# Up projection of a gated MLP as seven Strassen block products, and the down projection as a stage of its own

## The chip, the cores and the metric

The kernel runs on one core of one Trainium2 chip. The metric is the device time of one execution in microseconds (us): 1302.23 us, the median of three runs that lie between 1301.54 and 1302.39 us.

## The reference

One layer of a diffusion backbone: a token mixer (four recurrent heads and four Fourier groups) with a gated residual, then a gated MLP with a gated residual, then a last norm. The latents are 1024 tokens of 1024 features, all float32. The change lies in the MLP and around it:

```python
x = x + gt1 * (y @ w_out[l])
h2 = modulate(rms_norm(x, norm2[l]), sh2, sc2)
# conv_ffn, D_FF = 2816 hidden features, grid of 16 rows x 64 columns
a, u = jnp.split(h2 @ w_up, 2, axis=-1)
a = depthwise_conv_3x3(a) + b_dw
x = x + gt2 * ((jax.nn.gelu(a) * u) @ w_down)
return rms_norm(x, norm_f)
```

## The kernel before

Features lie on the 128 partitions and tokens along them. A page is a tile of 128 x 1024 float32. Every large product is done in three passes of TensorE: each operand is split into a rounded high part and the rest (ScalarE casts, line 62; VectorE subtracts, line 63), and high x high, high x low and low x high are summed in PSUM (`mm3`, line 76; `half_T`, line 285; all matmuls are recorded at line 74). A matmul has 128 columns of weights and 512 tokens.

`out_proj` (line 709) goes over the tokens in two halves and over eight feature tiles in each; it adds the residual into eight pages `x1` that stay in SBUF (line 727), sums squares, and then norms and modulates the half (`token_rstd` line 95, `row_bcast` line 103, `modulated` line 108) into the pages `h2`. While the second half is normed, TensorE does products of the first up projection with tokens of the first half (`half_T` on `up0`).

`ffn` (line 756) goes over 22 pairs `ff` of column tiles: 128 gate columns a and 128 columns u. Each is a product over eight feature tiles and two token halves, so 2 x 8 x 2 x 3 = 96 matmuls of 512 tokens a pair. The gate goes from PSUM into SBUF (line 774) and gets the centre tap on ScalarE (line 775), eight shifted taps on VectorE (line 783), GELU (line 785) and the product with u (line 793); the product is split for the next matmul. After every second pair, `down` (line 803) multiplies the two tiles by their rows of `w_down`: 96 matmuls, and 16 sums into `x1` on VectorE (line 812). The last group of two pairs is done in 512, 256 and 256 tokens, each followed by the last norm, transposes (line 835) and the store (`final`, line 816).

GpSimd does nothing in these stages. All transfers are issued from SyncE's queue (line 59). The order of the instructions on each engine is made when the program is built, by a list scheduler that takes the earliest ready instruction in program order; weight loads and their splits are put ahead (`wload` with `ahead`, line 65). At run time each engine follows its list in order.

Of the kernel before, what the change touches and what calls it, by code (L numbers as in the profile page):

```python
# [16 lines left out]
P = 128  # L17
D = 1024
L = 1024
# [15 lines left out]
class Kern:  # L35
# [59 lines left out]
    def token_rstd(self, ssacc, ntt, name, ptag="m"):  # L95
        """ssacc [128 features, ntt*128 tokens] -> rstd [128 tokens, ntt]"""
# [6 lines left out]
    def row_bcast(self, r, ntt, pt, off=0):  # L103
        """pt[:, off+j*128+t] = r[t, j] on every partition"""
# [11 lines left out]
    # ------------------------------------------------------------------ set-up  # L116
    def consts(self):
# [9 lines left out]
        self.mscan = c.tile([P, L], U8, tag="mscan", name="mscan")  # L127
# [5 lines left out]
        # for the first two rows of the modulation: stationary operands of 32 columns, two of them in use  # L133
# [8 lines left out]
        z = lambda n: c.tile([P, 512], F32, tag=n, name=n)  # L142
# [25 lines left out]
    def masks(self):  # L168
        nc, c = self.nc, self.sb["cst"]
# [9 lines left out]
    def mod_pair(self, ft):  # L179
        """shift and scale of feature tile ft for the first norm, of the latents and of the context"""  # L180
# [27 lines left out]
    def mod_part(self, part):  # L208
        """part 0..3: gt1, sh2, sc2, gt2"""
# [26 lines left out]
    # ------------------------------------------------------------------ first norm, zi  # L236
    def start(self):
        """The first norm in halves of 512 tokens; the values of the recurrent heads"""
# [22 lines left out]
        def square_sum(tiles, w, tag="sq"):  # L261
            """the last tile in pieces of w, which are added to the sum of the others"""
# [41 lines left out]
        # the clock of the tensor engine rises only when it is busy  # L304
# [52 lines left out]
        # context  # L357
# [38 lines left out]
    def half_T(self, pt, w, half, kts=(0, NK)):  # L396
        """one half of the tokens of an up projection, feature tiles kts"""
# [65 lines left out]
        # direction 0: half u of each chunk in row u; direction 1: in row 1 - u  # L463
# [8 lines left out]
        # states at the end of the context  # L472
# [42 lines left out]
        # scores  # L515
# [15 lines left out]
        # keys decayed to the end, queries from the start of each pair of chunks  # L531
# [10 lines left out]
        # chunk contributions to the states  # L542
# [20 lines left out]
        # outputs [tokens, values]  # L563
# [44 lines left out]
    def fnet(self):  # L608
# [27 lines left out]
        for g in range(4):  # L636
# [24 lines left out]
            # even and odd part; the last three rows mirror the rows 1 to 3 with the odd part negated  # L661
# [16 lines left out]
    # ------------------------------------------------------------------ gate of the recurrent heads  # L678
# [29 lines left out]
    # ------------------------------------------------------------------ output projection, second norm  # L708
    def out_proj(self):
        nc, V, I = self.nc, self.nc.vector, self.I  # L710
        self.x1 = [self.pg() for _ in range(NK)]
        order = [4, 5, 6, 7, 0, 1, 2, 3]
        h2 = None
        for half in range(2):
            s = slice(half * 512, (half + 1) * 512)
            ssacc = None
            for d in range(NK):
                if half == 0:
                    self.load(self.x1[d], I["xT"][d])
# [7 lines left out]
                V.scalar_tensor_tensor(self.x1[d][:, s], pt, self.gt1[:, d:d + 1], self.x1[d][:, s], op0=MUL, op1=ADD)  # L727
                sq = self.pg(F32, "zt")
                nc.scalar.activation(sq[:, :512], self.x1[d][:, s], AF.Square)
# [4 lines left out]
            if half == 1:  # L734
                w0 = [self.wload(I["wup"][0, 0], "pg", "pg"), self.wload(I["wup"][0, 1])]
                self.up0 = [self.pst("g"), self.pst("g")]
                self.half_T(self.up0[0], w0[0], 0)
            r = self.token_rstd(ssacc[:, :512], 4, "n2", "c")
            if half == 1:
# [223 lines left out]
```

## Time and profile before

| | |
|---|---|
| median of three runs | 1302.23 us |
| the profiled execution, first to last instruction (span) | 1301.3 us |
| TensorE matmuls, busy | 1265.0 us (97%) |
| VectorE, busy | 849.5 us (65%) |
| ScalarE, busy | 463.1 us (36%) |
| GpSimd, busy | 0.2 us (0%) |
| HBM traffic | 92.24 MB read, 4.19 MB written |

The profile is of one execution; its own time is the span, and the median of the runs lies 0.9 us above it. Matmuls overlap in the records, so TensorE's pace is read from the distance between starts, or from the length of an unbroken row of them. Weight loads are listed apart (PEld) and run beside the matmuls.

### The profile page before, as it was taken

How to read it: one execution, taken by the hardware profiler on the slowest of the kernel's cores; microseconds unless marked ns; L12 is line 12 of the kernel's file. 1: busy time of each engine (PE TensorE's matmuls, PEld its weight loads, DVE VectorE, ACT ScalarE, POOL GpSimd, SP SyncE). 2: the span in 40 equal slices, each digit the busy share in tenths (PEclk: the TensorE clock that was granted, in tenths of full speed). 3: DMA queues.
4: the chain of work that ended last, by engine and by line, in shares of the span. 5: the costliest groups of instructions: out<-in, count | busy, mean ns of one | idle time of the engine just before them, and what ended most of it. 6: DMA issues, size and time to landing. Idle time of an engine off the chain costs nothing.

```text
span 1301.3 us, 15784 instructions
## 1 busy us (share of the span) xinstructions
PE 1265.0 (97%) x6508; PEld 1060.9 (82%) x6508; DVE 849.5 (65%) x1172; ACT 463.1 (36%) x657; POOL 0.2 (0%) x4
## 2 busy tenths in 40 slices
PE   7999999999989999999999999999999999999996
PEld 4688887888988888888888888888888888888886
DVE  5843848476975664768656565656565656565776
ACT  6534463727132443444131313131313131313336
POOL 0000000000000000000000000000000000000000
PEclk9999999999999999999999999999999999999999
DMA  9531101101362354312121212121112121212103
GB/s 333 199 97 58 33 17 33 33 17 59 104 210 75 122 176 157 100 63 65 33 65 33 66 33 65 33 65 33 65 33 65 33 65 33 65 33 65 33 1 129
DMA packets 32503, 97.45 MB, mean 75 GB/s; under 512 B 3504, under 2 KB 3760, under 8 KB 32432
## 3 DMA queue, kind: packets, MB, share of 16 engines
q1 hardware_dynamic: 32432, 96.45, 22.7%
q8 instruction: 51, 0.84, 0.2%
q14 instruction: 20, 0.16, 0.0%
HBM read 92.24 MB, written 4.19 MB: 74 GB/s over the span
## 4 chain that ended last, share of the span: by engine, by line
PE 77%; ACT 10%; DVE 7%; DMA 3%; issue 2%; SPq 0%; DVEq 0%; ACTq 0%
PE psg L74 45%; PE psm L74 30%; DMA wm<-in_wm_dram 2%; DVE pg L459 1%; ACT sq L576 1%; ACT pg L822 1%; ACT L452 1%; ACT L453 1%; DMA ld<-in_wm_dram 1%; ACT zt L821 1%; ACT wh L62 1%; DVE ma L220 1%; ACT k L470 1%; ACT pg L452 1%; DVE zt L783 1%
## 5 line engine op out<-in xcount | busy, mean ns | idle before, releaser
L74 PE MATMUL psg<-pg,wh 128*128 128x512 f32 x1784 | 484.8, 391 | 0.6 <-ACT zt L775 0.6
L74 PEld LDWEIGHTS psg<-pg,wh 128*128 128x128 f32 x1784 | 333.4, 188 | 68.8 <-ACT zt L775 1.0
L74 PE MATMUL psg<-pg,wl 128*128 128x512 f32 x892 | 279.8, 391 | 0.0
L783 DVE SCALAR_TENSOR_TENSOR zt<-zt,vec,zt 128x945 f32<-128x945 f32 (+2 forms) x176 | 214.7, 1220 | 20.9 <-ACT zt L775 17.4
L63 DVE TENSOR_TENSOR wl<-wr,wh 128x1024 fp32r<-128x1024 f32 x79 | 96.6, 1223 | 193.8 <-ACT wh L62 192.6
L74 PEld LDWEIGHTS psg<-pg,wl 128*128 128x128 f32 x892 | 167.3, 188 | 34.1
L62 ACT CAST wh<-wr 128x1024 fp32r<-128x1024 f32 x79 | 82.9, 1050 | 304.9 <-PE psg L74 249.3
L812 DVE SCALAR_TENSOR_TENSOR pg<-psm,gt,pg 128x512 f32<-128x512 f32 (+1 forms) x184 | 130.2, 724 | 14.1 <-PE psm L74 12.9
L74 PE MATMUL psm<-gx,wd 128*128 128x512 f32 x480 | 135.1, 389 | 0.2 <-DVE gx L63 0.2
L74 PE MATMUL psm<-pg,wd 128*128 128x512 f32 x480 | 134.9, 389 | 0.0
L74 PEld LDWEIGHTS psm<-gx,wd 128*128 128x128 f32 x480 | 90.0, 188 | 19.2 <-DVE gx L63 0.6
L74 PEld LDWEIGHTS psm<-pg,wd 128*128 128x128 f32 x480 | 90.1, 188 | 18.7
L74 PE MATMUL psg<-wh,pg 128*128 128x256 f32 x512 | 97.5, 289 | 0.9 <-ACT wh L62 0.8
L62 ACT CAST wd<-wr 128x1024 fp32r<-128x1024 f32 x20 | 21.1, 1054 | 193.2 <-PE psm L74 164.3
L74 PEld LDWEIGHTS psg<-wh,pg 128*128 128x128 f32 x512 | 81.6, 194 | 1.6 <-ACT wh L62 1.3
L74 PE MATMUL psg<-wl,pg 128*128 128x256 f32 x256 | 73.7, 289 | 3.9 <-DVE wl L63 3.9
L74 PE MATMUL psm<-pg,pg 128*128 128x128 f32 (+2 forms) x328 | 71.8, 342 | 5.0 <-DVE pg L514 4.7
L74 PEld LDWEIGHTS psm<-pg,pg 128*128 128x128 f32 x328 | 51.9, 190 | 14.1 <-DVE pg L514 6.1
L74 PE MATMUL psg<-pg,pg 128*128 128x512 f32 x240 | 59.0, 395 | 1.2 <-ACT pg L113 1.2
L220 DVE SCALAR_TENSOR_TENSOR ma<-wm,silu_c,ma 128x512 f32<-128x512 f32 x56 | 42.0, 750 | 19.5 <-DMA wm<-in_wm_dram 19.2
L74 PEld LDWEIGHTS psg<-pg,pg 128*128 128x128 f32 x240 | 44.2, 188 | 12.6 <-ACT pg L113 2.2
L74 PEld LDWEIGHTS psg<-wl,pg 128*128 128x128 f32 x256 | 49.6, 194 | 4.6 <-DVE wl L63 4.5
(262 smaller groups left out, 1319.1 us busy)
## 6 DMA issues: line engine op xcount, KB each, us to landing
wr<-in_wup_dram SPq DMA_DIRECT2D x44, 512.0 KB, 3.5
wm<-in_wm_dram SPq DMA_DIRECT2D x64, 256.0 KB, 3.0
wr<-in_wd_dram SPq DMA_DIRECT2D x22, 512.0 KB, 3.5
ld<-in_wm_dram SPq DMA_DIRECT2D x16, 512.0 KB, 8.2
wr<-in_wo_dram SPq DMA_DIRECT2D x16, 512.0 KB, 3.5
pg<-in_xT_dram SPq DMA_DIRECT2D x12, 512.0 KB, 6.8
wr<-in_wT_dram SPq DMA_DIRECT2D x12, 512.0 KB, 3.6
out_dram<-wr SPq DMA_DIRECT2D x8, 512.0 KB, 2.6
```

Of the source, the lines that this page charges most:

```text
L62: self.nc.scalar.copy(hi, raw)
L63: self.nc.vector.tensor_tensor(lo, raw, hi.bitcast(F32), op=SUB)
L74: self.nc.tensor.matmul(out, lhsT, rhs, start=start, stop=stop)
L220: nc.vector.scalar_tensor_tensor(acc, w, s, acc, op0=MUL, op1=ADD)
L452: nc.scalar.activation(lf, g[d][0], AF.Ln)
L453: nc.scalar.activation(self.sm(1, "tab"), lf[:, 0:1], AF.Exp) # loads the table ahead
L459: V.tensor_tensor_scan(flip(lf, d), flip(lf, d), self.mscan, 0.0, op0=ADD, op1=MUL)
L470: nc.scalar.activation(kv[d], nat(st[d]["lf"]), AF.Exp, scale=-1.0)
L576: nc.scalar.activation(sq, o[:, blk(n)], AF.Square, accum_out=self.ssq[:, h * NT + n:h * NT + n + 1])
L783: V.scalar_tensor_tensor(c3[:, ro, co], a3[:, ri, ci], w9((dr + 1) * 3 + dc + 1), c3[:, ro, co], op0=MUL, op1=ADD)
L812: self.nc.vector.scalar_tensor_tensor(x[:, s], pt, self.gt2[:, d:d + 1], x[:, s], op0=MUL, op1=ADD)
L821: nc.scalar.activation(sq[:, :w], x[:, s], AF.Square)
```

## The change

For each pair, the weights are a 2 x 2 array of blocks: a or u, times the first or second 512 features. The normed input is a 2 x 2 array too: features halves times token halves (B11, B12, B21, B22). Their product is formed with seven block products instead of eight, in the form with shared sums: S1 to S4 are sums of weight blocks, U1 to U4 of input blocks. One block product is 4 x 3 = 12 matmuls of 512 tokens.

- `out_proj` keeps the residual stream in half pages that are written to DRAM (`x1d`, eight stores of 512 KB) and read back at the end. `norm2` forms raw blocks, splits of B11, B21, B22, and U1 to U4 with their splits. The pools of the MLP are opened between the halves' end and the second norm, and the first two products of pair 0 are issued ahead of that norm.
- `up_load` loads a pair's weights, forms the sums on GpSimd (four additions of 128 x 512 and one subtraction of 128 x 1024), and splits them.
- `ffn` does the seven products into three PSUM banks, with three copies to SBUF on ScalarE and three sums on VectorE. The gate stays in PSUM and the taps read it there. The gated page goes to DRAM (`gd`, 22 stores of 512 KB).
- `down` runs after all pairs: it loads gated halves back and splits them, and sums over all 22 pairs in PSUM. The first token half goes in two sweeps over four feature tiles with 512 tokens (528 matmuls), the second in two sweeps over eight feature tiles with 256 tokens (1056 matmuls), each with its own load and split of the weights. `final` follows each part.
- Tables of the recurrence stage move to a pool that is closed before the MLP. Comments are gone.

```diff
+    def norm2(self, half, xs, ssacc):
...
+            self.phase("ffn")
+            self.up_first()
+        r = self.token_rstd(ssacc[:, :512], 4, "n2", "g")
...
+        for j in range(2):
+            b12 = block("B12", j, 2 * j, False)
+            b22 = block("B22", j, 4 + 2 * j)
+            u1, u2 = self.pg(F32, "cv"), self.pg()
+            V.tensor_tensor(u1, self.raw["B11"][j], b12, op=SUB)
+            V.scalar_tensor_tensor(u2, u1, -1.0, b22, op0=MUL, op1=SUB)
+            operand("U2", u2)
+            operand("U1", u1)
...
+            G.tensor_tensor(s31[:, hi], u[:, lo], u[:, hi], op=ADD)
+            G.tensor_tensor(s24[:, lo], s31[:, hi], a[:, lo], op=ADD)
+            G.tensor_tensor(s24[:, hi], s24[:, lo], a[:, hi], op=ADD)
+            G.tensor_tensor(s31[:, lo], a[:, lo], u[:, lo], op=ADD)
+            S24 = self.pg(F32R, "sh"), self.pg(F32R, "sl")
+            self.split(s24, *S24)
+            S31 = self.pg(F32R, "sh"), self.pg(F32R, "sl")
+            nc.scalar.copy(S31[0], s31)
+            G.tensor_tensor(S31[1], s31, S31[0].bitcast(F32), op=SUB)
+            A22 = self.tile([P, 512], F32R, "ah"), self.tile([P, 512], F32R, "al")
+            self.split(u[:, hi], *A22)
...
+                X, Y = self.pst("m"), self.pst("m")
+                self.product(X, w["A11"], "B11", True)
+                s1 = snap(X)
+                self.product(Y, w["A12"], "B21", True)
+            pa = self.pst("g")
+            V.tensor_tensor(pa[:, h0], s1, Y, op=ADD)
+            self.product(X, w["S2"], "U2", False)
+            sv = snap(X)
+            Z = self.pst("m")
+            self.product(Z, w["S1"], "U1", True)
+            s5 = snap(Z)
+            self.product(X, w["S3"], "U3", False)
+            u = self.pg(F32, "uu")
+            V.scalar_tensor_tensor(u[:, h1], X, -1.0, s5, op0=MUL, op1=SUB)
+            self.product(Z, w["S4"], "B22", False)
+            V.tensor_tensor(pa[:, h1], sv, Z, op=ADD)
+            self.product(X, w["A22"], "U4", False)
+            nc.scalar.mul(u[:, h0], X, -1.0)
             if ff + 1 < NF:
-                nxt = [self.wload(I["wup"][ff + 1, j]) for j in range(2)]
-            if len(pend) == 2 and ff < NF - 2:
-                self.down(pend)
+                self.upw.append(self.up_load(ff + 1))
+            cv = self.pg(F32, "cv")
...
-            nc.scalar.copy(a, pa)
             nc.scalar.activation(cv, pa, AF.Identity, bias=v[:, V_BDW + ff:V_BDW + ff + 1], scale=w9(4))
...
+            V.tensor_tensor(cv, cv, u, op=MUL)
+            g = self.tile([P, 1024], F32, "gd")
+            self.load(g, cv)
+            self.gd.append(g)
+        self.down()
...
-    "ffn": (dict(zt=5, wd=4, gx=4), dict(m=4)),
+    "ffn": (dict(wx=2, ws=2, sh=2, sl=2, ah=1, al=1, cv=2, uu=1, sn=4), dict(m=4)),
```

In the last lines the numbers are buffers: one page for u (`uu`), two for the gate (`cv`), two each for the split sums (`sh`, `sl`, one pair's worth), two for raw sums (`ws`). The general pool of pages has 30, before and after.

## Rows read from the trace of the kernel before

**Rows 1.** The page of the profile, part 1: span and engines
```profile
span 1301.3 us, 15784 instructions
...
PE 1265.0 (97%) x6508; PEld 1060.9 (82%) x6508; DVE 849.5 (65%) x1172; ACT 463.1 (36%) x657; POOL 0.2 (0%) x4
```

**Rows 2.** The chain that ended last, in order of time: start us, us, engine, lines
```profile
617.20 20.93 PE psm L74 x91
638.13 43.52 PE psg L74 x192
681.65 21.76 PE psm L74 x96
```

**Rows 3.** Who waited for whom between 640 and 1236 us, longest first: top rows
```profile
ACT wh L62 <- PE psg L74: 203.9, 36, 9.3
DVE wl L63 <- ACT wh L62: 166.8, 27, 9.6
```

**Rows 4.** Busy time of the engines in stretches
```profile
core 0: us, PE busy (x) PEld busy (x) DVE busy (x) ACT busy (x) POOL busy (x), PEclk, DMA share, GB/s
488.00:560.00 72.00, 71.91 (x326) 59.63 (x327) 45.26 (x63) 28.20 (x37) 0.00 (x0) 1.00 0.40 129
...
640.00:770.00 130.00, 130.00 (x575) 107.69 (x574) 82.64 (x85) 32.59 (x32) 0.00 (x0) 1.00 0.16 49
1259.00:1301.30 42.30, 32.11 (x221) 28.39 (x219) 29.24 (x65) 29.49 (x56) 0.00 (x0) 0.93 0.24 100
```

**Rows 5.** TensorE's timeline around the second norm
```profile
558.49 5.60 PE L74 MATMUL psg<-pg,pg 128*128 128x512 f32 x24
563.93 1.05 PE L74 MATMUL psc<-ones,zt 128*128 128x128 f32 x8
```

**Rows 6.** Groups of instructions by line and shape, ScalarE: busy us, mean ns
```profile
L62 ACT CAST wh<-wr 128x1024 fp32r<-128x1024 f32 x79 | 82.9, 1050 | 304.9 <-PE psg L74 249.3 <-PE psm L74 39.7 <-issue 11.5
...
L775 ACT ACTIVATE zt<-psg,vec 128x1024 f32<-128x1024 f32 x22 | 26.6, 1209 | 0.0
...
L785 ACT ACTIVATE zt<-zt 128x1024 f32<-128x1024 f32 x22 | 23.3, 1058 | 30.7 <-DVE zt L783 30.6
```

**Rows 7.** VectorE's timeline around the second norm and the first pairs
```profile
568.73 2.06 DVE L112 SCALAR_TENSOR_TENSOR zt<-pg,a,psc 128x512 f32<-128x512 f32 x3 [1.31 <-PE psc L74]
...
585.19 8.79 DVE L783 SCALAR_TENSOR_TENSOR zt<-zt,vec,zt 128x960 f32<-128x960 f32 x7
```

**Rows 8.** Groups of instructions by line and shape again, VectorE
```profile
L812 DVE SCALAR_TENSOR_TENSOR pg<-psm,gt,pg 128x512 f32<-128x512 f32 x168 | 122.8, 747 | 12.8 <-PE psm L74 11.7
...
L63 DVE TENSOR_TENSOR wl<-wr,wh 128x1024 fp32r<-128x1024 f32 x79 | 96.6, 1223 | 193.8 <-ACT wh L62 192.6
...
L459 DVE TENSOR_TENSOR_SCAN pg<-pg,mscan 128x1024 f32<-128x1024 f32 x8 | 18.3, 2292 | 11.2 <-ACT tab L453 11.2
...
L510 DVE SCALAR_TENSOR_TENSOR k<-zt,oml,k 128x512 f32<-128x512 f32 x16 | 11.6, 745 | 0.0
...
L733 DVE TENSOR_TENSOR zt<-zt,zt 128x512 f32<-128x512 f32 x14 | 9.6, 686 | 0.1
```

**Rows 9.** DMA issues on the page: KB each, us to landing
```profile
wr<-in_wup_dram SPq DMA_DIRECT2D x44, 512.0 KB, 3.5
...
out_dram<-wr SPq DMA_DIRECT2D x8, 512.0 KB, 2.6
```

**Rows 10.** TensorE's timeline in the last group: start us, us, line, shape, count
```profile
1289.70 0.52 PE L74 MATMUL psm<-pg,pg 128*128 128x256 f32 x3
1290.06 0.53 PE L74 MATMUL psm<-gx,pg 128*128 128x256 f32 x3
1290.42 1.33 PE L835 MATMUL psg<-ident,pg 128*128 128x128 f32 x10
```

**Rows 11.** The page of the profile, part 2: GB/s in 40 slices of the span
```profile
GB/s 333 199 97 58 33 17 33 33 17 59 104 210 75 122 176 157 100 63 65 33 65 33 66 33 65 33 65 33 65 33 65 33 65 33 65 33 65 33 1 129
```

More of the change, by code (lines that the diff above doesn't have):

```diff
@@ L168, in masks @@
     def masks(self):
-        nc, c = self.nc, self.sb["cst"]
+        nc, c = self.nc, self.sb["cm"]
         mk = self.pg(F32, "ld")[:, :4 * P]
@@ L742, in out_proj @@
[L742 to L753 removed]
+                if d % 2:
+                    t = self.x1d[half, d // 2] = self.tile([P, 1024], F32, "x1d")
+                    self.load(t, x)
@@ new lines, in up_load @@
+    def up_load(self, ff):
+        nc, I, G = self.nc, self.I, self.nc.gpsimd
+        lo, hi = slice(0, 512), slice(512, 1024)
+        with self.tc.high_priority():
+            a, u = self.pg(F32, "wr"), self.pg(F32, "wx")
+            self.load(a, I["wup"][ff, 0])
+            self.load(u, I["wup"][ff, 1])
+            A = self.pg(F32R, "wh"), self.pg(F32R, "wl")
+            self.split(a, *A)
+            s24, s31 = self.pg(F32, "ws"), self.pg(F32, "ws")
+            G.tensor_tensor(s31[:, hi], u[:, lo], u[:, hi], op=ADD)
[9 more added lines that the diff above has]
+            self.split(u[:, hi], *A22)
+        cut = lambda t, s: (t[0][:, s], t[1][:, s])
+        return dict(A11=cut(A, lo), A12=cut(A, hi), S2=cut(S24, lo), S4=cut(S24, hi), S3=cut(S31, lo), S1=cut(S31, hi),
+                    A22=A22)
@@ new lines, in product, with up_first @@
+    def product(self, out, w, name, first):
+        B = self.B[name]
+        for kt in range(4):
+            q, t = slice(kt * P, (kt + 1) * P), slice((kt % 2) * 512, (kt % 2 + 1) * 512)
+            for j, (a, b) in enumerate(((0, 0), (0, 1), (1, 0))):
+                self.nc.tensor.matmul(out, w[a][:, q], B[kt // 2][b][:, t], start=(first and kt == 0 and j == 0),
+                                      stop=(kt == 3 and j == 2), skip_group_check=not first)
+    def up_first(self):
+        self.upw = [self.up_load(ff) for ff in range(1)]
+        self.upp = []
+        for w in self.upw:
+            X, Y = self.pst("m"), self.pst("m")
+            self.product(X, w["A11"], "B11", True)
+            self.product(Y, w["A12"], "B21", True)
+            self.upp.append((X, Y))
@@ new lines, in ffn, with copied, g_load @@
+            g = self.tile([P, 1024], F32, "gd")
+            self.load(g, cv)
+            self.gd.append(g)
+        self.B = None
+        self.down()
+    def copied(self, dst, src):
+        self.nc.scalar.copy(dst, src)
+        return dst
+    def g_load(self, half):
+        gs = []
+        for i in range(NF // 2):
+            raw = self.pg(F32, "ws")
+            for j in range(2):
+                self.load(raw[:, j * 512:(j + 1) * 512], self.gd[2 * i + j][:, half * 512:(half + 1) * 512])
+            hi, lo = self.pg(F32R), self.pg(F32R)
+            self.split(raw, hi, lo)
+            gs.append((hi, lo))
+        return gs
@@ new lines, in sweep, with step @@
+    def sweep(self, pages, load, pts, g, t, cut):
+        tail = []
+        n = len(pages)
+        def step(i, hi, lo, j):
+            c = pages[i][1]
+            for k in range(c * i, c * i + c):
+                gh, gl = g[k // 2]
+                tt = slice((k % 2) * 512 + t.start, (k % 2) * 512 + t.stop)
+                w = cut(k, j)
+                for m, (a, b) in enumerate(((hi, gh), (hi, gl), (lo, gh))):
+                    bank0 = len(pts) == 4 or j % 2 == 0
+                    nc = self.nc
+                    nc.tensor.matmul(pts[j], a[:, w], b[:, tt], start=(k == 0 and m == 0 and bank0),
+                                     stop=(k == NF - 1 and m == 2), skip_group_check=len(pts) != 4)
+        for i in range(n):
+            hi, lo = load(i)
+            if i < n - 2:
+                for j in range(len(pts)):
+                    step(i, hi, lo, j)
+            else:
+                tail.append((i, hi, lo))
+        for j in range(len(pts)):
+            for i, hi, lo in tail:
+                step(i, hi, lo, j)
@@ new lines, in resid, with final @@
+    def resid(self, x, pt, d):
+        self.nc.vector.scalar_tensor_tensor(x, pt, self.gt2[:, d:d + 1], x, op0=MUL, op1=ADD)
+    def final(self, xs, t0, w):
+        nc, V = self.nc, self.nc.vector
+        ssacc = self.pg(F32, "cv")[:, :w]
+        for d, x in enumerate(xs):
+            if d == 0:
+                nc.scalar.activation(ssacc, x, AF.Square)
+            else:
+                sq = self.pg(F32, "cv")[:, :w]
+                nc.scalar.activation(sq, x, AF.Square)
+                V.tensor_tensor(ssacc, ssacc, sq, op=ADD)
+            nc.scalar.activation(x, x, AF.Copy, scale=self.vec[:, V_NF + d:V_NF + d + 1])
+        tag = "g" if w == 512 else "m"
+        r = self.token_rstd(ssacc, w // P, "nf", tag)
+        for i in range(w // P):
+            t = slice(i * P, (i + 1) * P)
+            ob = self.pg(F32, "uu")
+            for h in range(2):
+                pt = self.pst(tag)[:, :512]
+                for j in range(4):
+                    nc.tensor.transpose(pt[:, j * P:(j + 1) * P], xs[4 * h + j][:, t], self.ident)
+                o = ob[:, h * 512:(h + 1) * 512]
+                if h:
+                    V.tensor_scalar(o, pt, r[:, i:i + 1], None, op0=MUL)
+                else:
+                    nc.scalar.activation(o, pt, AF.Copy, scale=r[:, i:i + 1])
+            self.load(self.out[t0 // P + i], ob)
```

219 lines of the change are left out of this document (124 added, 95 removed).

## The prediction

> **What bounds the kernel now.** First the page: TensorE is busy 97% of the span, VectorE 65%, GpSimd not at all [rows 1]. A busy TensorE need not be the limit, so the chain that ended last comes next: from 617 us on it is one unbroken row of matmuls, 192 of a pair of up projections in 43.52 us, then 96 of a down group in 21.76 us, and so on to the last group [rows 2]. Both give 0.2267 us a matmul of 512 tokens. The list of waits agrees: the long ones are ScalarE and VectorE waiting for TensorE, and TensorE is not among the waiters [rows 3]. The stretches say the same: 130.00 us of 130 at the full granted clock, VectorE at 82.64 [rows 4]. So from 558.49 us, the first matmul of the up projection [rows 5], to the end, time is counted in matmuls, and the change pays only by removing some of them while nothing else becomes late. Before that point nothing changes on TensorE: it is busy 71.91 of 72 us in the output projection [rows 4], with VectorE at 45.26 and ScalarE at 28.20, and the eight extra half-page ScalarE passes for raw blocks of the first half (each under a page cast's 1.05 us [rows 6]) and the stores of 512 KB fit beside that. I cost them at nothing; without that cover they would cost at most 8 us.
>
> **The up projection.** Removed: 12 of 96 matmuls in each of 22 pairs, 264 x 0.2267 = 59.8 us. What remains is 84 x 0.2267 = 19.04 us a pair, 418.9 us in all. The question is whether the other engines keep up with 19.04 us, since the 10.88 us of down matmuls that used to lie beside each pair are gone from this stage.
>
> VectorE per pair: eight taps, which seven in a row show at 8.79 us together [rows 7], so 10.0 us for eight. They now read PSUM; a 512-column form of this operation takes 747 ns from PSUM and 745 ns from SBUF [rows 8], so I add nothing. Three page-wide subtractions or products (splits of the a weights and of S2/S4, the gate product) at 1.223 us: 3.7. Three half-page ones (the split of A22, two sums into the gate) at 0.686: 2.1. One half-page sum for u, 0.75. Together 16.5 of 19.04 us, 87%. The sums into `x1` are gone from here. ScalarE has three page casts, one half-page cast, four half-page PSUM copies, the centre tap 1.21 and GELU 1.06 [rows 6]; with a half page taken as high as a page it would still be under 11 us.
>
> Throughput holds, so the chain matters. VectorE, in order, must finish for pair n: the second gate sum after the sixth product (0.69), then the centre tap on ScalarE (1.21), eight taps (10.0), with the split of A22 (0.69) and of a later a (1.22) between them, GELU (1.06), the gate product (1.22). Only then is the single page for u free, and the u row of pair n+1 (0.75) must have read its bank before the seventh product of n+1 may write it. That is 16.8 us plus some 0.4 for handing over between engines: 17.2, where TensorE allows 19.04. The slack is 1.8 us.
>
> GpSimd has no row here that shows an addition. Bounds: at least VectorE's own time for the same sizes [rows 8], 4 x 0.686 + 1.223 = 4.0 us a pair; at most the slowest page-wide form on VectorE, the scan at 2.292 us a page [rows 8], 4 x 1.15 + 2.29 = 6.9 us. I take the upper end, so that a slow engine is not overlooked. Either way it fits into 19 us: the raw sums have two buffers and are formed a pair ahead. By the Trainium skill (GPSIMD Engine Reference, "Elementwise — side-by-side cycle accounting") an addition of 2048 float32 takes 4497 ns there, an estimate of 6.7 us for these five; the sum would be the same. What GpSimd can cost is delay to VectorE. If each of the split of S2/S4 and the split of A22, which come right when GpSimd starts its next sums, waits about half a microsecond, the slack is nearly used up; I take a loss of 0.4 us a pair, 9 us, between 0 and 2 us a pair (0 to 44).
>
> The three copies of partial sums must be done before the next write into the same bank, one product or 2.72 us later; a half-page copy needs well under a page cast's 1.05 us, so they cost nothing unless ScalarE is held behind another wait. SyncE has three transfers a pair in place of three: two weight loads, 3.5 us to landing, and a store like the output's, 2.6 us [rows 9]. Loads queued behind a store that waits for the gate product are a pair ahead, which covers them.
>
> **The start.** Before, TensorE went on with first-half products while the second half was normed. Now it has two products, 24 x 0.2267 = 5.44 us, then the norm's small matmuls at 563.93 [rows 5]; VectorE begins to modulate at 568.73 [rows 7], as before. From there it does 12 half-page passes (three take 2.06 us [rows 7]: 8.2 us), eight page sums for U1 to U4 and eight subtractions for their splits (16 x 1.22 = 19.5), and splits of S2/S4 and A22 (1.9): 29.6 us, to 598.3. The last half of the seventh product ends 1.4 us later, at 599.7. Matmuls alone would have ended at 558.5 + 19.04 = 577.5, so 22.2 us are lost; one product of pair 1 (2.7 us) can be done in the gap, as a fourth bank is free. Loss 19.5 us; at least 10 if more is brought forward and passes overlap, at most 27 if casts on ScalarE come into the row.
>
> **The step to the down stage.** After the sixth product of the last pair VectorE still has taps, GELU wait and product, some 14 us; TensorE has the seventh product, 2.7, and, with the first gated pages and weights split ahead, one page of 24 matmuls, 5.4. The next split of weights comes behind the taps. I take 5 us lost, between 0 and 11 (14 less 2.7). The last gated page needs its store and load back, some 6 us [rows 9], and is not used before the tenth page, 49 us on.
>
> **The down stage.** First half: 528 x 0.2267 = 119.7 us. Second half: 1056 of 256 tokens. In the last group of before, three of these start every 0.36 us [rows 10], 0.12 us each, more than half of 0.2267: 126.7 us. VectorE has a gated split and a weight split in each 5.44 us, or one weight split in 2.88 us, so it is covered. A weight page of 512 KB in 2.88 us is 182 GB/s; the first slice of before moved 333 [rows 11], so I cost the loads, which each go out ahead into four buffers, at nothing. Ahead of the last part go 48 transposes and small matmuls, at 0.13 us each [rows 10] some 7 us. From the last product at 1290.59 us the tail of before took 10.7 us to the end of the span [rows 1, 10]; the new one has the same steps with 256 tokens: 11 us.
>
> **The sum.** 558.5 + 418.9 + 19.5 + 9 + 5 + 119.7 + 126.7 + 7 + 11 = 1275.3 us against the profiled span of 1301.3, the profiled execution's own time. The median of the runs is 0.9 us more, so 1276 us.
>
> **Rivals.** *All of it fits.* The chain keeps its 1.8 us slack, and start and step cost 14 and 2 in place of 19.5 and 5: 1276 - 9 - 8.5 = 1258 us. For it: VectorE has 87% of a pair and the plain rows are start to start a little shorter than their durations. Against: 1.8 of 19 us is little for a chain that changes engines five times in every pair.
>
> *VectorE's chain becomes the bound, with GpSimd in its way.* Four VectorE operations a pair read two pages of SBUF (three splits, the gate product). If each waits for one GpSimd addition of half a page, 1.15 us by the scan's row, the chain is 17.2 + 4.6 = 21.8 us, 2.8 over TensorE, 61 us in 22 pairs in place of my 9: 1276 + 52 = 1328 us, slower. It decides from a pair of about 20.7 us on, where the 26 us and the 9 us allowed are gone (35/22 = 1.6 over 19.04). For it: the slack is small. Against: the taps, the largest part, read one operand from PSUM, and the sums are bunched in under half of a pair. Beside it stands a rule of the Trainium skill (SBUF — State Buffer, "SBUF: two separate sides"): the port pair that VectorE and GpSimd share is an exclusive lock, taken by a VectorE operation with two SBUF inputs or by a GpSimd one for its whole length, and the other blocks. No run here shows it yet.
>
> *The edges eat the gain.* The start at 27 and the step at 11, and the second half's first gated pages late by as much again (11): 1276 + 7.5 + 6 + 11 = 1300 us, no change. For it: pages are tight (28 of 30 hold the input blocks). Against: gated pages come free one by one in the second sweep.
>
> **Chances.** About 0.2% of the time, 2.6 us, is what a measurement of this kernel can tell from no change. Forecast 0.56, all fits 0.18, VectorE's chain 0.17, edges 0.09, of which 0.03 a little faster, 0.04 the same and 0.02 a little slower. Faster 0.77, same 0.04, slower 0.19. The range takes in the case that all fits with 5 us below it, and upwards a loss of 1.7 us a pair: 1253 to 1305; outside stay most of the chain's case and a corner below.
>
> **What would show it.** Right: 264 fewer matmuls of 512 in the stage, a pair every 19.0 to 19.6 us in the chain, TensorE idle some 20 us between 565 and 600, VectorE above 80% in the stage, 0.12 us a matmul in the last 127 us. Wrong: a chain through VectorE's taps in every pair, subtractions of a page well above 1.22 us beside GpSimd, pairs of 20.7 us or more, or gaps of over 10 us between the stages.

## The result, and the profile after

The changed kernel takes 1310.36 us, the median of four runs between 1310.10 and 1313.72 us. The kernel before, run beside it, takes 1302.31 us (1301.54 to 1305.28, four runs). The ratio is 1.0064, with a 95% interval from 1.0047 to 1.0080: slower by 0.6%, where 1276 us and a range up to 1305 us were forecast.

The page of the changed kernel, part 1; the same two lines of before are [rows 1]:

```profile
span 1308.4 us, 17010 instructions
...
PE 1227.5 (94%) x6724; PEld 1042.5 (80%) x6724; DVE 904.0 (69%) x1160; ACT 570.4 (44%) x813; POOL 178.8 (14%) x114
```

TensorE has 37.5 us less to do and the span is 7.1 us longer, so some 45 us of idle time are new. Its timeline shows where, with the time it sat idle and the releaser in brackets (rows of other stretches left out). The 566.94 is the first matmul of the up projection, which stood at 558.49 [rows 5]; at 670.40 the fourth pair is done (338 matmuls of 512 tokens, 84 a pair and the first two of the fifth); at 1153.21 the second token half of the down projection begins, and the last row of a down product starts at 1291.15.

```profile
535.68 1.19 PE L74 MATMUL psm<-k,wh 128*128 128x512 f32 x2 [4.96 <-DVE pg L731]
...
566.94 0.70 PE L839 MATMUL psm<-pg,wh 128*128 128x512 f32 x2 [0.94 <-ACT wh L62]
...
576.91 2.08 PE L74 MATMUL psg<-ident,n2r 128*128 128x128 f32 x8 [3.39 <-DVE n2r L92]
...
593.61 0.79 PE L839 MATMUL psm<-pg,sh 128*128 128x512 f32 x1 [14.63 <-ACT pg L761]
...
670.40 0.39 PE L839 MATMUL psm<-pg,wl 128*128 128x512 f32 x1
...
1034.40 0.74 PE L839 MATMUL psm<-pg,ah 128*128 128x512 f32 x2 [1.37 <-DVE uu L876]
...
1038.81 0.73 PE L987 MATMUL psm<-pg,wh 128*128 128x512 f32 x2 [1.36 <-ACT uu L880]
...
1153.21 0.40 PE L987 MATMUL psm<-pg,wh 128*128 128x256 f32 x2
...
1175.40 1.06 PE L1023 MATMUL psg<-ident,pg 128*128 128x128 f32 x8 [2.35 <-DVE uu L1026]
...
1291.15 0.28 PE L987 MATMUL psg<-pg,sl 128*128 128x256 f32 x1
...
1297.43 1.20 PE L74 MATMUL psm<-ones,cv 128*128 128x128 f32 x4 [6.00 <-DVE cv L1013]
```

With these marks the span can be set against the prediction's sum, term by term:

| term | predicted, us | measured, us | difference |
|---|---|---|---|
| first up matmul | 558.5 | 566.94 | +8.4 |
| lost at the start: 670.40 - 566.94, less 338 matmuls of 0.2267 | 19.5 | 26.9 | +7.4 |
| lost in the other 18 pairs | 9 | 18.1 | +9.1 |
| step to the down stage, 1.37 + 1.36 | 5 | 2.7 | -2.3 |
| second token half with norms and transposes, 1153.21 to 1291.43 | 133.7 | 138.2 | +4.5 |
| tail, 1291.43 to 1308.4 | 11 | 17.0 | +6.0 |
| all | | | +33.1 |

The third line is worked out from the rest: from 566.94 to 1153.21 are 586.3 us, the up projection and the first down half have 538.6 us of matmuls, and of the 47.7 us between, 26.9 and 2.7 have their own lines. The sum of 1275.3 and the span of 1308.4 differ by the same 33.1.

The stretches tell the same story (columns as in [rows 4]):

```profile
516.00:560.00 44.00, 39.04 (x166) 31.86 (x165) 26.47 (x38) 20.01 (x29) 0.00 (x0) 0.92 0.48 164
...
582.00:600.00 18.00, 6.39 (x15) 4.65 (x16) 18.00 (x18) 10.64 (x16) 7.77 (x5) 0.51 0.10 30
...
640.00:1000.00 360.00, 348.43 (x1520) 283.83 (x1519) 311.62 (x273) 147.91 (x182) 141.85 (x90) 1.00 0.22 81
```

Where [rows 4] had 130.00 us of 130, TensorE now has 348.43 of 360 between 640 and 1000 us, with VectorE at 87%. Between 582 and 600 us it was busy for 6.39 of 18 us, and the granted clock was 0.51, its lower level of 1.2 GHz: 11.6 us of the wait of 14.63 lie in this stretch, and behind it fourteen matmuls, from 593.61 to 599.92, start 0.45 us apart and not 0.2267. That alone is 3.1 us.

**The pair.** This is the timeline of one pair in the middle of the stage: start us, us, engine, line, tiles, shape; `al` is the low part of A22, `sl` of line 827 that of S3 and S1 (GpSimd's subtraction), `sl` of line 63 that of S2 and S4.

```profile
785.00 0.69 DVE L876 SCALAR_TENSOR_TENSOR uu<-psm,sn 128x512 f32<-128x512 f32 x1
785.61 1.21 DVE L63 TENSOR_TENSOR sl<-ws,sh 128x1024 fp32r<-128x1024 f32 x1
...
786.74 0.69 DVE L878 TENSOR_TENSOR psg<-sn,psm 128x512 f32<-128x512 f32 x1
...
786.90 1.30 POOL L819 TENSOR_TENSOR ws<-wx 128x512 f32<-128x512 f32 x1 [12.21 <-DVE sl L63]
...
788.15 1.30 POOL L822 TENSOR_TENSOR ws<-wr,wx 128x512 f32<-128x512 f32 x1
...
788.71 1.20 DVE L893 SCALAR_TENSOR_TENSOR cv<-psg,vec,cv 128x945 f32<-128x945 f32 x1 [1.28 <-ACT cv L885]
...
789.40 2.41 POOL L827 TENSOR_TENSOR sl<-ws,sh 128x1024 fp32r<-128x1024 f32 x1
...
789.83 2.53 DVE L63 TENSOR_TENSOR al<-wx,ah 128x512 fp32r<-128x512 f32 x1
...
791.89 1.62 POOL L820 TENSOR_TENSOR ws<-ws,wr 128x512 f32<-128x512 f32 x1
...
792.28 5.05 DVE L893 SCALAR_TENSOR_TENSOR cv<-psg,vec,cv 128x960 f32<-128x960 f32 x4
...
797.25 0.69 DVE L868 TENSOR_TENSOR psg<-sn,psm 128x512 f32<-128x512 f32 x1
...
797.84 1.22 DVE L63 TENSOR_TENSOR wl<-wr,wh 128x1024 fp32r<-128x1024 f32 x1
...
798.98 3.69 DVE L893 SCALAR_TENSOR_TENSOR cv<-psg,vec,cv 128x945 f32<-128x945 f32 x3
...
802.76 1.06 ACT L895 ACTIVATE cv<-cv 128x1024 f32<-128x1024 f32 x1 [2.40 <-DVE cv L893]
...
803.85 1.23 DVE L896 TENSOR_TENSOR cv<-cv,uu 128x1024 f32<-128x1024 f32 x1 [1.19 <-ACT cv L895]
...
805.19 0.69 DVE L876 SCALAR_TENSOR_TENSOR uu<-psm,sn 128x512 f32<-128x512 f32 x1
...
805.94 0.73 PE L839 MATMUL psm<-pg,ah 128*128 128x512 f32 x2 [0.82 <-DVE uu L876]
```

The split of A22 starts at 789.83, while GpSimd is in the middle of its page-wide subtraction, and ends at 792.36, 0.55 us after that subtraction (791.81). It takes 2.53 us where the same operation alone takes 0.69 (the first gate sum, line 868, has as many columns). GpSimd's next addition pays too, 1.62 us where the one before took 1.30. The tap at 788.71, which has one operand in PSUM, runs beside an addition of GpSimd and takes 1.20 us like any other. Everything on VectorE comes 1.84 us later, down to the u row at 805.19, and TensorE's seventh product waits for that row. The pair before had it at 785.00, so a pair takes 20.19 us and not 19.04.

By the groups it is the rule and not this one pair:

```profile
L893 DVE SCALAR_TENSOR_TENSOR cv<-psg,vec,cv 128x945 f32<-128x945 f32 x88 | 105.6, 1200 | 25.4 <-ACT cv L885 23.9
...
L827 POOL TENSOR_TENSOR sl<-ws,sh 128x1024 fp32r<-128x1024 f32 x22 | 54.0, 2455 | 35.0 <-ACT sh L826 35.0
...
L63 DVE TENSOR_TENSOR al<-wx,ah 128x512 fp32r<-128x512 f32 x22 | 44.9, 2043 | 4.2 <-ACT ah L62 4.2
L820 POOL TENSOR_TENSOR ws<-ws,wr 128x512 f32<-128x512 f32 x22 | 35.5, 1615 | 1.5
```

**The edges.** At the second norm the sums of pair 0 and then of pair 1 lie across VectorE's row:

```profile
575.38 1.26 POOL L820 TENSOR_TENSOR ws<-ws,wr 128x512 f32<-128x512 f32 x1
575.47 1.19 DVE L91 SCALAR_TENSOR_TENSOR n2t<-n2t,n2r 128x4 f32<-128x4 f32 x1
...
584.78 2.29 DVE L63 TENSOR_TENSOR wl<-wr,wh 128x1024 fp32r<-128x1024 f32 x1
585.94 2.24 POOL L820 TENSOR_TENSOR ws<-ws,wr 128x512 f32<-128x512 f32 x1
586.98 3.41 DVE L778 SCALAR_TENSOR_TENSOR pg<-sn,sh,pg 128x512 fp32r<-128x512 f32 x2
```

An operation on four columns, line 91, takes 1.19 us (0.16 in the run below without GpSimd's additions), and two half-page ones, line 778, take 3.41 us together; later ones take 0.74 each. In the tail the last part's output goes through one page:

```profile
1288.59 1.66 DVE L1002 SCALAR_TENSOR_TENSOR sn<-psg,gt,sn 128x256 f32<-128x256 f32 x4 [6.46 <-PE psg L987]
...
1291.66 1.66 DVE L1002 SCALAR_TENSOR_TENSOR sn<-psg,gt,sn 128x256 f32<-128x256 f32 x4
...
1301.19 3.90 SPq L59 DMA_DIRECT2D out_dram<-uu  x2
...
1303.90 0.69 ACT L1028 ACTIVATE uu<-psm,nfr 128x512 f32<-128x512 f32 x1 [3.27 <-DMA out_dram<-uu]
```

The second tile of tokens waits 3.27 us for the store of the first, since `uu` has one page. The wait of 2.35 us at 1175.40 is the same in the part before. The norm's first matmul stands at 1297.43, 6.0 us after the last product's end at 1291.43. In the kernel before it followed after 2.75 us (from 1290.59, [rows 10]):

```profile
1293.34 0.71 PE L74 MATMUL psm<-ones,zt 128*128 128x128 f32 x4 [0.33 <-DVE zt L826]
```

### The profile page after: what moved, and what is told of

It is laid out like the page before. It is cut to its first block, busy times and chain, and to the rows that moved or that the text cites. A ratio compares the mean times of both kernels' runs of the same rounds, so it can differ in the third digit from the quotient of the medians.

```text
span 1308.4 us, 17010 instructions
## 1 busy us (share of the span) xinstructions
PE 1227.5 (94%) x6724; PEld 1042.5 (80%) x6724; DVE 904.0 (69%) x1160; ACT 570.4 (44%) x813; POOL 178.8 (14%) x114
## 4 chain that ended last, share of the span: by engine, by line
PE 50%; DVE 26%; ACT 12%; issue 6%; DMA 5%; POOL 0%; SPq 0%; DVEq 0%; ACTq 0%; POOLq 0%
PE psm L74 13%; PE psg L74 10%; DVE cv L893 9%; PE psm L987 9%; PE psg L987 9%; PE psm L839 7%; DVE al L63 3%; DMA wm<-in_wm_dram 2%; DVE wl L63 2%; DVE sl L63 2%; DVE cv L896 2%; ACT cv L885 2%; ACT cv L895 1%; DVE pg L460 1%; DMA ws<-gd 1%
## 5 line engine op out<-in xcount | busy, mean ns | idle before, releaser
L893 DVE SCALAR_TENSOR_TENSOR cv<-psg,vec,cv 128x945 f32<-128x945 f32 (+2 forms) x176 | 214.7, 1220 | 27.5 <-ACT cv L885 23.9
L839 PE MATMUL psm<-pg,sh 128*128 128x512 f32 x704 | 219.3, 393 | 14.9 <-ACT pg L761 14.6
L839 PEld LDWEIGHTS psm<-pg,sh 128*128 128x128 f32 x704 | 133.0, 189 | 44.2 <-ACT pg L761 15.2
L839 PE MATMUL psm<-pg,sl 128*128 128x512 f32 x352 | 137.6, 391 | 0.0
L74 PE MATMUL psg<-pg,wh 128*128 128x512 f32 x408 | 115.1, 395 | 0.0
L839 PE MATMUL psm<-pg,wh 128*128 128x512 f32 x352 | 109.2, 391 | 0.9 <-ACT wh L62 0.9
L74 PEld LDWEIGHTS psg<-pg,wh 128*128 128x128 f32 x408 | 75.3, 188 | 14.5
L839 PEld LDWEIGHTS psm<-pg,sl 128*128 128x128 f32 x352 | 66.7, 189 | 13.9
L839 PE MATMUL psm<-pg,wl 128*128 128x512 f32 x176 | 68.5, 389 | 0.0
L74 PE MATMUL psg<-pg,wl 128*128 128x512 f32 x204 | 66.7, 396 | 0.0
```

The costliest lines, as they stand in the source:

```text
L74: self.nc.tensor.matmul(out, lhsT, rhs, start=start, stop=stop)
L839: self.nc.tensor.matmul(out, w[a][:, q], B[kt // 2][b][:, t], start=(first and kt == 0 and j == 0), stop=(kt == 3 and j == 2), skip_group_ ...
L893: V.scalar_tensor_tensor(c3[:, ro, co], a3[:, ri, ci], w9((dr + 1) * 3 + dc + 1), c3[:, ro, co], op0=MUL, op1=ADD)
```

## The experiments

Each ratio is to the kernel before, run beside it; its median there lay between 1304.32 and 1304.53 us.

**The lock theory.** VectorE's split of A22 is held while GpSimd's subtraction runs; without that, 19.04 us a pair fit. If so, the split goes to the engine that does the subtraction:

```diff
-            self.split(u[:, hi], *A22)
+            nc.scalar.copy(A22[0], u[:, hi])
+            G.tensor_tensor(A22[1], u[:, hi], A22[0].bitcast(F32), op=SUB)
```

> Theory (lock): in the changed kernel the split of A22 on VectorE takes 2.04 us in place of 0.69, because it waits for GpSimd's page-wide subtraction, and this lies on the chain that sets a pair at 20.2 us. With the low part of A22 formed on GpSimd instead, VectorE's chain loses these 2.0 us and TensorE bounds the pair again: 19.0 to 19.3 us a pair, 1286 to 1291 us in place of 1310. Rival (late operand): GpSimd now has six operations in a row, the low part of A22 comes behind them, and the seventh product waits for it instead: a pair stays at 20 us or more, 1306 us or more. Rival (taps): the taps and hand-overs alone make the chain longer than 19.04: a pair of 19.6 to 20, 1298 to 1306.

Measured: 1290.2 us (1288.09 to 1292.04), ratio to the kernel before 0.9886 (0.9859 to 0.9913). The stretch that had 348.43 of 360 and the moved operation:

```profile
640.00:1000.00 360.00, 360.00 (x1589) 298.18 (x1588) 292.60 (x267) 156.32 (x193) 163.51 (x111) 1.00 0.26 90
...
L830 POOL TENSOR_TENSOR al<-wx,ah 128x512 fp32r<-128x512 f32 x22 | 28.6, 1298 | 5.3 <-ACT ah L829 5.3
```

TensorE is never idle in it and a pair takes 19.04 us. GpSimd is busy for 21.66 us more of this stretch and VectorE for 19.02 less. The time is in the expected range, and neither rival came. So the split's place was the cause of the longer pair. It could still be that VectorE merely had too much to do, so the next run leaves the split where it was and leaves out GpSimd's four additions (raw weight blocks are split in place of their sums, so what it forms is no longer the layer's product):

```diff
-            s24, s31 = self.pg(F32, "ws"), self.pg(F32, "ws")
-            G.tensor_tensor(s31[:, hi], u[:, lo], u[:, hi], op=ADD)
-            G.tensor_tensor(s24[:, lo], s31[:, hi], a[:, lo], op=ADD)
-            G.tensor_tensor(s24[:, hi], s24[:, lo], a[:, hi], op=ADD)
-            G.tensor_tensor(s31[:, lo], a[:, lo], u[:, lo], op=ADD)
+            s24, s31 = a, u
```

> Leaves out GpSimd's four additions of weight blocks (raw weight blocks are split in their place); the page-wide subtraction stays on GpSimd. Theory (lock): the subtraction then runs right behind its cast and is over before the split of A22 starts, which takes 0.7 us; a pair falls to 19.0 to 19.3 us; at the second norm VectorE's stretched rows (3.4, 2.3, 2.0 us) go back to their lengths, which gives 4 to 7 us more: 1279 to 1285 us. Rival (taps): VectorE's rows are stretched for another reason, or the chain is too long without that: a pair stays at 19.8 or more, and the time at 1300 or more.

Measured: 1286.79 us (1285.13 to 1287.54), ratio 0.9859 (0.9833 to 0.9884), pairs of 19.04 us with the same work on VectorE:

```profile
L63 DVE TENSOR_TENSOR al<-wx,ah 128x512 fp32r<-128x512 f32 x22 | 16.9, 769 | 0.8 <-ACT ah L62 0.3
```

The split is back at 769 ns in the mean, as the subtraction no longer falls on it. So the amount of work on VectorE was not the cause. The time is 1.8 us above the expected range; the first up matmul stands at 570.01 in this run, 3.1 us later than in the changed kernel. The start lost less. The seventh product of the fifth pair, 408 matmuls behind the first, begins at 682.79 us, so that 20.3 us are lost up to there; in the changed kernel it begins at 686.27, with 26.8 lost (26.2 to 27.8 in the other runs that have the additions where they were). So some 6.5 us of that term go with GpSimd's additions.

**Lock or shared port.** A port that both share in proportion would explain the two runs as well. Here the subtraction is cut into two, with the same work beside the split:

```diff
-            G.tensor_tensor(S31[1], s31, S31[0].bitcast(F32), op=SUB)
+            for q in (lo, hi):
+                G.tensor_tensor(S31[1][:, q], s31[:, q], S31[0][:, q].bitcast(F32), op=SUB)
```

> The changed kernel with one edit: GpSimd's page-wide subtraction (the low part of S3 and S1) is issued as two subtractions of 512 columns; the split of A22 stays on VectorE. Same work, half the length of the longest GpSimd instruction. Theory (a VectorE operation with two SBUF inputs is held until the GpSimd instruction that runs has ended): the split of A22 waits for the first half alone, takes 1.2 to 1.6 us in place of 2.53, and the pair falls from 20.18 to between 19.04 and 19.3 us, the time to 1285 to 1293 us. Rival 1 (both engines share a port and slow each other in proportion while both run): the total of GpSimd's work beside the split is the same, the split stays near 2.5 us and the time near 1310. Rival 2 (GpSimd starts its second half at once and keeps VectorE out): the split ends with the second half, 2.6 us or more, time 1310 to 1314.

Measured: 1293.61 us (1293.01 to 1297.35), ratio 0.9926 (0.9909 to 0.9943), 360.00 of 360 us busy between 640 and 1000 us. One pair in the timeline:

```profile
784.97 3.00 POOL L828 TENSOR_TENSOR sl<-ws,sh 128x512 fp32r<-128x512 f32 x2
785.84 0.98 DVE L63 TENSOR_TENSOR al<-wx,ah 128x512 fp32r<-128x512 f32 x1
```

The split waits for the rest of the first half only and takes 0.98 us, and now the second half waits for the split: the two take 3.00 us together where the whole took 2.41. These are turns of a whole instruction. Slowing in proportion does not give 2.53 us in one kernel and 0.98 in the other, with the same work beside the split; and the second half did not keep the split out. Both rivals of this run fall. The split came out shorter than expected and the time 0.6 us above the expected range.

By the Trainium skill (SBUF — State Buffer, "SBUF: two separate sides") the port pair of VectorE and GpSimd is a lock that one instruction holds to its end, taken by a VectorE operation with two SBUF inputs against a GpSimd one that reads SBUF; the four durations above (2.53, 1.62, 0.98 and 3.00 us) agree, and so does the tap with a PSUM input, which was not held.

**The gap in the output projection.** The 4.96 us at 535.68 wait for line 731, the first residual sum of the second half. Its load went out at 528.17 us and landed at 532.48; line 731 began at 534.79, as VectorE, in its order, had steps of the first half's blocks to do before it. If the load is late because its page of the general pool comes free late, pages taken in advance end the gap. Here all eight are taken and loaded ahead of the two halves:

```diff
         for half in range(2):
             s = slice(half * 512, (half + 1) * 512)
+            xs = [self.pg() for _ in range(4)]
+            halves.append(xs)
+            for i, x in enumerate(xs):
+                self.load(x.rearrange("p (k t) -> p k t", k=2), I["xT"][2 * i:2 * i + 2, :, s].rearrange("k p t -> p k t"))
+        for half in range(2):
...
-                if d % 2 == 0:
-                    x = self.pg()
-                    xs.append(x)
-                    self.load(x.rearrange("p (k t) -> p k t", k=2), I["xT"][d:d + 2, :, s].rearrange("k p t -> p k t"))
+                x = xs[d // 2]
```

> Both halves of the residual input are loaded ahead of the first half. Theory (page): TensorE's gap of 4.96 us in the second half of the output projection is the wait for a load that had no free page until the blocks of the first half gave one back; with the page taken earlier the gap goes, the up projection starts at 559 to 561 us in place of 567, and the time is 1302 to 1305 us. Rival (busy VectorE and ScalarE): the sums out of PSUM are late because both engines are full with the blocks of the first half; the gap stays at 4 us or more, and the time at 1308 to 1311.

Measured: 1302.49 us (1300.0 to 1305.61), ratio 0.9983 (0.9967 to 0.9999). The gap is gone, so the rival falls (a gap of 4 us or more was its sign). But the edit moves the loads both to other pages and to another place in SyncE's queue, where the late one stood right behind a weights load that went out at 527.79; which of the two held it is not shown. The stretch that had 39.04 of 44 at 0.92 is full:

```profile
516.00:560.00 44.00, 44.00 (x203) 36.48 (x203) 31.23 (x44) 24.10 (x34) 0.00 (x0) 1.00 0.40 133
```

The first up matmul comes at 562.90, later than the expected 559 to 561; the time is in the expected range. Pairs still take 20.18 us. The traces show what the 8.4 us are made of. The 192 matmuls ahead of the first up matmul take 51.28 us in the changed kernel (from 515.66) and 42.11 in the kernel before (from 516.38): 9.2 us more, of which the earlier start hides 0.7. 5.1 of these are the wait. Behind it fourteen matmuls, from 535.68 to 541.78, start 0.44 us apart, at a granted clock of 0.50 (1.2 GHz): 2.9 us. The last 1.1 is the wait for the cast of the first up weights (0.94 in the row at 566.94). With the early loads the same 192 take 43.20 us, here and in the runs below, so that only this 1.1 is left; where they begin differs from run to run, between 515.65 and 519.70, with nothing changed ahead of them.

**The output page.** The store wait in the tail, tried the short way:

```diff
-            ob = self.pg(F32, "uu")
+            ob = self.pg()
```

> Output tiles take a page of the general pool in place of the single page for u. Theory (single page): at the end the second output tile waits 3.3 us for the store of the first; with a page of its own the end comes 2.5 to 3.5 us sooner, 1307 to 1308 us. Rival: the last store ends no sooner, because the two transfers run one behind the other anyway: 1310 us.

Measured: 1317.3 us (1316.15 to 1319.58), ratio 1.0100 (1.0069 to 1.0131): a miss, no faster than the changed kernel and rather slower (the intervals of the two ratios touch). The wait for the store is gone, and this stands in the middle of the stage in its place (TensorE's timeline of this run):

```profile
1159.62 2.08 PE L74 MATMUL psg<-ones,cv 128*128 128x128 f32 x8 [5.26 <-DVE cv L1013]
...
1169.01 0.74 PE L987 MATMUL psm<-pg,wh 128*128 128x256 f32 x4 [1.14 <-ACT pg L62]
```

The output pages of the first half compete with the gated pages for the general pool, and the gated splits of the second half come late. That the page was missing is read from the releasers; it was not tested by itself. A later run, with other pages for the last part alone, has no such row.

**Together.** A22 on GpSimd and the early loads:

> The low part of A22 on GpSimd and the residual input loaded ahead, together. If the two losses are separate, they add: 20 us for the pairs and 8 us before the up projection, so 1282 us, a pair of 19.04 us, and no gap in the output projection. Rival: the second half's norm is what sets the start, and an earlier end of the output projection only makes it wait longer: 1287 to 1290 us.

Measured: 1284.51 us (1282.09 to 1286.08), ratio 0.9842 (0.9824 to 0.9860), pairs of 19.04 us, and no gap in the output projection; 2.5 us above the sum that was expected. The start still has a wait of 14.69 us for U2. So, with both edits, the sums of pair 1 are made to come after U4, by a copy of one column that the first sum overwrites:

```diff
+            if ff == 1:
+                nc.scalar.copy(s31[:, 512:513], self.u4[:, 0:1])
             G.tensor_tensor(s31[:, hi], u[:, lo], u[:, hi], op=ADD)
```

> As both, and GpSimd's sums for the second pair wait until the last input block sum of the second norm is formed. Theory (lock at the start): VectorE's stretched rows at the second norm (3.4, 2.3 and 2.0 us) are waits for these sums; without them the first pairs end 2 to 4 us sooner: 1278 to 1280 us. Rival: the sums for the first pair are what stretches them, or the sums come late for the second pair: no gain, 1282 us or more.

Measured: 1278.35 us (1277.38 to 1281.88), ratio 0.9806 (0.9789 to 0.9824). TensorE's wait at the same place:

```profile
584.13 0.79 PE L847 MATMUL psm<-pg,sh 128*128 128x512 f32 x1 [11.61 <-ACT pg L765]
```

It is 3.1 us shorter, and the two half-page operations that took 3.41 us take 1.40 again. The opposite, pair 1's weights and sums made even earlier so that its first products fill the gap:

```diff
-        self.upw = [self.up_load(ff) for ff in range(1)]
+        self.upw = [self.up_load(ff) for ff in range(2)]
...
-            if ff + 1 < NF:
-                self.upw.append(self.up_load(ff + 1))
+            if ff + 2 < NF:
+                self.upw.append(self.up_load(ff + 2))
```

> As both, with the first two products of the second pair issued ahead of the second norm as well (24 matmuls, 5.4 us). Theory (TensorE short of work at the start): of some 28 us lost there, 15 are a wait for the first split of U2; two more products fill 2.7 to 5.4 us of it: 1277 to 1280 us. Rival: with two pairs' banks held, the third bank of the first pair comes late, or the loads two pairs ahead wait for buffers: no gain or slower, 1282 us or more.

Measured: 1295.85 us (1291.24 to 1296.26), ratio 0.9927 (0.9908 to 0.9947): a miss. ScalarE and VectorE take their instructions in order, and splits that wait for GpSimd's sums now stand before the norm; TensorE waits 9.40 us for it (timelines of the three engines):

```profile
571.49 1.04 ACT L62 CAST sh<-ws 128x1024 fp32r<-128x1024 f32 x1 [5.84 <-POOL ws L825]
572.56 1.23 DVE L63 TENSOR_TENSOR sl<-ws,sh 128x1024 fp32r<-128x1024 f32 x1 [11.26 <-ACT sh L62]
...
580.89 2.07 PE L74 MATMUL psg<-ident,n2r 128*128 128x128 f32 x8 [9.40 <-DVE n2r L92]
```

The output page again, with both edits and for the last part alone, when gated pages are no longer taken:

```diff
-            ob = self.pg(F32, "uu")
+            ob = self.pg(F32, "uu") if t0 < 768 else self.pg()
```

> As both, with output pages of the general pool for the last 256 tokens alone. Theory (single page at the end): the second output tile no longer waits 3.3 us for the store of the first, and nothing ahead of it changes: 2.5 to 3.5 us sooner, 1279 us. Rival: pages of the general pool are short, as in the run with all output tiles there, and the end comes later: 1284 us or more.

Measured: 1279.41 us (1278.55 to 1283.51), ratio 0.9816 (0.9796 to 0.9835), in the median 5.1 us under the kernel with both edits, though the intervals overlap. In the two traces the tail is 1.9 us shorter (16.9 to 15.1). The second half of the down stage is shorter too, by 3.5 us, with no wait of 2.40 us for an output page in it; the edit changes the pages of the last part alone, so not all of the 5.1 us can be put down to it. Finally all four edits:

> The changed kernel with four edits together: A22's low part on GpSimd, the residual loads ahead of the halves, the sums of pair 1 held until U4 is formed, and output tiles of the last part from the general pool. If the gains lie on separate stretches they add: 1278.35 us of the first three less the 3.3 us wait for the store gives 1275 us, between 1273 and 1278; first up matmul near 560, pairs of 19.04 us, no wait of a tile for a store in the tail. Rival: the end is set by the chain of sums, norm and copies in the last part and not by the store, so that the wait moves to another step there: 1278 us or more, as the output tiles alone gave nothing against 1279 in the earlier pair of runs.

Measured: 1277.7 us (1276.26 to 1281.65), ratio 0.9803 (0.9785 to 0.9821), span 1276.3. The wait for the store is gone and the tail is 14.6 us, where the changed kernel had 17.0, so the rival's wait that moves elsewhere in the tail is not seen. But against the run with the later sums and the old output page (0.9806) nothing is gained that can be told: that run lost 24.9 us between its first up matmul and the second down half, over the 538.6 us of matmuls, and this one 27.5. TensorE had 47.52 us of 50 at a clock of 0.97 between 590 and 640 us here, and 48.50 at 1.00 there. The trace has the place: in both runs TensorE waits twice just before 609 us (1.14 and 0.53 us here, 0.97 and 0.53 there), and here nine matmuls behind the second wait, from 608.47 to 612.17, start 0.41 us apart, at a granted clock of 0.77 between 610 and 615 us. That is 1.7 us, and a wait of 0.59 us at 628.18 is most of the rest. Why the clock fell here and not there is open.

## Why the prediction was wrong

**The matmuls: right.** TensorE does a pair in 19.04 us as soon as nothing holds it, and the last 432 matmuls of 256 tokens form a row of 51.84 us, 0.12 us each. The loads of the down stage cost nothing, and the step to it 2.7 us, in the range of 0 to 11.

**The step that failed is "I take a loss of 0.4 us a pair".** It rested on two sizes. The chain on VectorE was put at 17.2 us and a slack of 1.8. From start to start, the timeline above gives 20.19 us; less the 1.84 us by which the split of A22 is late, that is 18.35. The working had left out two operations that stand between the named ones, the first gate sum and the split of S2 and S4, 0.59 and 1.13 us from start to start; what it did name came out 0.6 us shorter than priced. So the slack was 0.7 us. And the delay was taken as half a microsecond for each of two splits; it is 1.84 us for one of them and none for the other, which GpSimd waits for before it starts (12.21 us in the row at 786.90). The rest is a loss of 1.15 us a pair, 18.1 us in 18 pairs, where 9 us in 22 were allowed. These parts of the 20.19 us are read from one timeline; that a slack was there is shown by the runs in which the split takes 0.77 or 0.98 us and a pair 19.04. The 0.4 us did not follow from the working's own sizes either: two delays of half a microsecond are 1.0, less than a slack of 1.8. That a wait lasts until a whole instruction of GpSimd has ended stood in a rival alone.

**The rival with GpSimd in the way had the mechanism** and the wrong count: it let four operations wait 1.15 us each; one waits, for a longer instruction. Pairs of 20.7 us, from which it was to decide, were not reached. In the pairs alone it cost 18.1 us, 9.1 more than the forecast has for them, which by itself gives some 1285 us and not a slower kernel. Its removal there agrees: 1310.36 to 1290.2 us, 20 us.

**Slower it was made by the edges**, 24.0 us over their terms in the table, and 6.5 of these are GpSimd in VectorE's way once more:
- *The output projection was costed at nothing*, with at most 8 us without its cover. It took 9.2 us more than in the kernel before, above that bound too, and the reason given for zero was of another kind: it counted work on ScalarE and stores. But the loads of the second half now go out late. The residual pages are held until the norm has made its blocks; with pages and loads ahead of the halves the gap is gone, though the runs don't tell the page from the place in the queue. TensorE's 71.91 of 72 us [rows 4] said nothing on pages, and the 2.9 us at the lower clock behind the gap had no term.
- *The start* took 26.9 us, where 19.5 was the value and 27 the end of its range. Of the excess of 7.4, some 6.5 us go with GpSimd's additions (the run without them); when those of pair 1 alone are moved, the wait for U2 is 3.1 us shorter. The working had GpSimd in the pairs and not at the start, where VectorE is busy without a break (18.00 of 18 us). The product of pair 1 that was to fill 2.7 us of the gap did not run in it: TensorE has nothing to do in the 14.63 us. And the fourteen matmuls at the lower clock, 3.1 us, had no term.
- *The second half and the tail* took 4.5 and 6.0 us more. The waits of 2.35 and 3.27 us for one output page were not in the sum; "the same steps with 256 tokens" overlooked that the residual is now added by fours after the last sum in PSUM (1.66 us each), with squares and scalings behind them. TensorE waits 6.00 us for these, 3.2 us longer than before; this and the store's 3.27 us are about the tail's excess over the 10.7 us of before.

**How it was put together.** The lock and the edges were rivals of each other, each priced from the same forecast with all else as planned. Nothing excludes both, and both came: 9.1 and 24.0 us. Their sum had no case of its own, so 1308 lay outside the range although the pairs (0 to 44) and the start (up to 27) lay inside their bounds. With the four edits that the runs led to, the kernel takes 1277.7 us, 1.97% less than the kernel before (1.79 to 2.15%): about what was forecast for the change as it stood.

## What to carry to other kernels

Before work goes to GpSimd, list the VectorE operations with two operands in SBUF that can meet it, let each wait for the longest GpSimd instruction and not for a share of it, and shorten that instruction or move the one that meets it to GpSimd as well. Sum a chain through several engines from every instruction in the order of its engines, those that belong to other work too: here two forgotten ones, 0.6 and 1.1 us, were most of a slack of 1.8. Unfavourable terms that don't exclude each other are added up in one case before the range is set, with buffers that are held longer (pages, here) costed like an engine.

## What the runs showed of the hardware

- GpSimd adds 128 x 512 float32 in 1.26 to 1.30 us when nothing holds it, and subtracts a page of 128 x 1024 in 2.41: nearly twice VectorE's 0.69 and 1.22. A pair's five operations are some 7.5 us, more than the upper bound of 6.9 that the slowest page-wide form of VectorE [rows 8] gave. The total changed nothing, as GpSimd has 19 us. By the Trainium skill (GPSIMD Engine Reference, "Elementwise — side-by-side cycle accounting") the estimate was 6.7 us, low as well.
- The lock doesn't ask for size: VectorE's operations on 128 x 4, 0.16 us alone, took up to 1.19 us beside an addition of GpSimd, and GpSimd's own took 2.24 in place of 1.26 us between two of VectorE's.
- A wait of TensorE can cost more than its length. Behind the wait of 14.63 us fourteen matmuls ran at a granted clock of 0.51 (1.2 GHz), 3.1 us more than at 0.2267 us each; behind the one of 4.96 us fourteen ran at 0.50, 2.9 us more. With that wait gone, the clock of the same stretch of 44 us was 1.00 and not 0.92.
